# Mixer scores with one 128-row stationary operand, and the small steps of a threshold search on GpSimd

## Chip, cores and metric

One core of a Trainium2 chip runs the whole program in one launch. The metric is the device time of one execution in microseconds, as the median of several runs.

## What is computed

A decoder block on 1024 tokens of width 1024 (one layer, batch 1): a mixer of three kinds of attention, cross attention to 256 memory tokens, a gated MLP with a short convolution, and a last norm. The change lies in the mixer:

```
h = rmsnorm(x, norm_mix)
aq, ak, av, bq, bk, bv, cq, ck, cv, iq, ik, iw = split(h @ w_in)
A: 4 heads, two softmax maps of 64 columns each, minus lam times the second
B: 4 heads of 64 columns, dilated windows
C: indexer: score[t,s] = sum_h iw[t,h] * relu(iq[t,h] . ik[s] / 8)      (8 heads of 64 columns)
   the 256 best keys s <= t of each t are kept; 4 heads of 64 columns attend to them alone
x = x + concat(A, B, C) @ w_out
...
s = q . k * scale + bias[bucket(t - s)];   p = softmax(s);   o = p @ v
```

Products are made from float32 numbers split into a high part (float32r) and a low part, the rest: q = qh + ql, k = kh + kl.

## The kernel before, in words

`build_mixer` (L293) writes the mixer as strands, generators that yield pieces of work for an engine with an estimated duration. The class `Flow` (L60) runs them as a list schedule: of the work that is ready for an engine, the lowest rank goes first, and the order so found is the order in which the instructions are issued on TensorE, ScalarE, VectorE and GpSimd, and the transfers on SyncE. Each engine then runs its queue strictly in that order; a table `LAG` holds the estimated hand-over times. `Slots` are counters of free buffers, `Gate`s are events.

Projections: for each unit u (two heads, or one head of A with its two maps) `project_k`, `project_v` and `project_q` (L607, L629, L587) make the transposed keys, the values and the queries, in two halves of 512 tokens, each half from 24 matmuls with 512 moving columns (three passes, `mm3`, L174 to L176, for each of eight chunks). Keys of the next unit are projected beside the scores of this one (`kk_s` has two slots). ScalarE copies the high part out of PSUM, VectorE subtracts to get the low part. For the queries the transfers issued by SyncE (L158) build `qs`, whose 128 rows are, for each of the two heads, [high; low] of its 64 columns; `qh` keeps the high parts of both heads in their own rows. For the keys they build `kd`, [high; high] of each head; the low parts `kl` stay where VectorE wrote them, 64 rows a head.

Scores: `scores_mm` (L705) makes a chunk of up to 512 keys for 128 queries in two passes into one PSUM bank. The first, L709, takes `qs` against `kd` over 128 rows: qh.kh + ql.kh. The second, L710, takes 64 rows of `qh` against 64 rows of `kl`: qh.kl. It is used by the indexer (`index_chunk`, tile psi, 80 chunks) and by all heads (`scores_all`, tile pss, 192 chunks). `index_keys` (L666) has one head of keys, and makes its copies in both halves of the rows itself.

Evacuation: VectorE adds the bias strip and finds the maximum in one pass (`evacuate`, shown as CUSTOM_DVE, with its accumulator read as `nm`), ScalarE takes the exponentials; `turn_all` transposes, `values_all` multiplies with the values.

Search: `selection` (L775) finds the 256th best score of each row bit by bit, 16 bits of the high halves and 16 of the low ones, for two sets of row blocks: blocks 2 to 5 count on VectorE (suffix d, four counts a bit), blocks 6 and 7 on ScalarE (suffix a, two counts a bit). After the counts of a bit three small VectorE instructions on 128x4 or 128x2 elements set the next threshold (`sel_g`, `sel_thr`, then `sel_lo`). `rank()` paces the search to an end at 505 us of the schedule's own clock. Where masks are ready, the scores of units 6 and 7 add them by a third matmul (L895).

GpSimd has, in this part, the low parts of the weights (`wl`, 128x512, L117, the line of every recorded strand) in the same order of issue.

Of the kernel before, what the change touches and what calls it, by code (L numbers as in the profile page):

```python
# [14 lines left out]
F32 = mybir.dt.float32  # L15
F32R = mybir.dt.float32r
# [8 lines left out]
P = 128  # L25
# [34 lines left out]
class Flow:  # L60
    """Decides the order in which the engines get their instructions: a list schedule over a small model
    of the engines. A strand is a generator that yields (engine, us, emit[, rank]) for work, a time to
    let pass, a Gate to wait for, or Slots to take one of; the lowest rank goes first. Work that several engines
    can do goes to the one that would be done with it first."""
# [86 lines left out]
def trunk(ctx, tc, a, out):  # L151
# [3 lines left out]
    def rdma(dst, src):  # L155
        """Copies float32r bits."""
        f = lambda t: t.bitcast(F32) if t.dtype == F32R else t
        nc.sync.dma_start(f(dst), f(src))  # L158
# [5 lines left out]
    # ---------------------------------------------------------------- helpers  # L164
# [13 lines left out]
    def load_w(pool, w, c, n=P, parts=1, eng=nc.gpsimd):  # L178
        """128 columns of a weight matrix, split: lists of [128, n] by chunk of rows."""
# [13 lines left out]
    def rsqrt(v, n, between):  # L193
        """1 / sqrt(v) for a tile of n columns, with other work between its steps."""
# [30 lines left out]
    def transposed_split(src, dst_h, dst_l, col, trp, tag="tr"):  # L225
        """src [128 rows, 1024] into dst[:, chunk, col:col+128], split."""
        for q in range(2):
            ps = trp.tile([P, 4, P], F32, tag=tag, name="tr")
            for j in range(4):
                c = (4 * q + j) * P  # L230
                nc.tensor.transpose(ps[:, j, :], src[:, c : c + P], ident)
            dh = dst_h[:, 4 * q : 4 * q + 4, col : col + P]
            nc.scalar.activation(dh, ps, AF.Copy)
            nc.vector.tensor_tensor(dst_l[:, 4 * q : 4 * q + 4, col : col + P], ps, dh.bitcast(F32), OP.subtract)

    # -------------------------------------------------------------- constants
# [8 lines left out]
    # DRAM scratch  # L245
# [12 lines left out]
    def w_half(w, half, name, pool, stp):  # L258
        """512 columns of a weight matrix, split."""
# [33 lines left out]
    def build_mixer():  # L293
# [5 lines left out]
        vt_s, pt_s, o_s, t_s, w_s, st_s = Slots(2), Slots(2), Slots(2), Slots(2), Slots(3), Slots(2)  # L299
        go, put, open_ = flow.go, flow.put, flow.open  # L300

        def move(us, *fs, rank=None):
            """Transfers as strand work."""
# [13 lines left out]
        def rstd_ops(ss, width, n, res):  # L317
            """The steps of 1 / sqrt(ss / width + eps) as strand work."""
# [19 lines left out]
        # ------------------------------------------------ weights of columns  # L338
# [53 lines left out]
        # ------------------------------------------------ rows, normalised and transposed  # L392
# [12 lines left out]
        class Rows:  # L405
            """Blocks of rows that share the steps to their inverse norms."""
# [10 lines left out]
        def row_block(rows, j, t):  # L417
            """A block of rows: loaded, normalised, transposed, split."""
# [58 lines left out]
        def all_rows():  # L477
            """Memory first: its projection fills the time that the tokens need."""
# [8 lines left out]
        def keep_clock():  # L487
            """Fills the array's pauses before the first long run of products, so that its clock stays up."""
# [10 lines left out]
        # ------------------------------------------------ bias vectors by distance, lambda  # L499
# [46 lines left out]
        def load_strips():  # L546
            """The biases of a head, skewed by row: 128 copies a row apart by one."""
# [23 lines left out]
        # ------------------------------------------------ projections  # L571
# [15 lines left out]
        def project_q(key, u, scale):  # L587
            """Transposed projection of two heads, by half: high parts, and [high; low] of each head."""
            hd = heads[u]

            def finish(half, ps):
                yield vt_s
                qh = hp.tile([P, 512], F32R, tag="qh", name="qh", bufs=3)
# [8 lines left out]
                hd.q[half] = (qh, qs)  # L602
# [4 lines left out]
        def project_k(key, u):  # L607
            """Transposed projection of two heads: low parts, and [high; high] of each head."""
            hd = heads[u]

            def finish(half, ps):
                yield vt_s
                sl = slice(512 * half, 512 * half + 512)
                kh = pp.tile([P, 512], F32R, tag="vt", name="kh")
                yield ACT, act(512), partial(nc.scalar.activation, kh, ps, AF.Copy)
                yield DVE, dve(512), partial(nc.vector.tensor_tensor, hd.kl[:, sl], ps, kh.bitcast(F32), OP.subtract)
                put(pj_s)
                r = [slice(0, 64), slice(64, 128)]
                yield from move(1.46, *(copy(hd.kd[r[x], m, sl], kh[r[m]]) for m in range(2) for x in range(2)))
                put(vt_s)  # L620
                hd.k = hd.kl, (hd.kd[:, 0], hd.kd[:, 1])
# [3 lines left out]
            hd.kl = hp.tile([P, S], F32R, tag="kl", name="kl")  # L625
# [3 lines left out]
        def project_v(key, u):  # L629
            """Values in their natural layout, [high | low] for each head."""  # L630
# [34 lines left out]
        # ------------------------------------------------ indexer  # L665
        def index_keys():  # L666
            hd = heads["ik"]

            def finish(half, ps):
                yield vt_s  # L670
                kl, kh = hd.kl, hd.kd[:, 0]
# [7 lines left out]
                hd.k = kl, (kh, kh)  # L679
# [15 lines left out]
            hd.kl = hp.tile([P, S], F32R, tag="kl", name="ikl")  # L695
# [3 lines left out]
        def chunks_of(n):  # L699
            """Columns by bank, none under half of one where that can be helped."""  # L700
# [4 lines left out]
        def scores_mm(ps, q, k, m, qb, c0, n, stop=True):  # L705
            qh, qs = q[qb // 4]
            c = slice(qb % 4 * P, qb % 4 * P + P)
            r = slice(64 * m, 64 * m + 64)
            nc.tensor.matmul(ps[:, :n], qs[:, m, c], k[1][m][:, c0 : c0 + n], start=True, stop=False)  # L709
            nc.tensor.matmul(ps[:, :n], qh[r, c], k[0][r, c0 : c0 + n], start=False, stop=stop)  # L710
# [43 lines left out]
        # ------------------------------------------------ the 256 best keys of each row  # L754
# [5 lines left out]
        def keys(b):  # L760
            """Ordered 16-bit keys of the scores: high halves, low halves (as stored)."""
# [13 lines left out]
        def selection(blocks, on_act, end):  # L775
            """The 256th best score of each row, bit by bit: of the high halves, then of the low ones of
            the scores that share that high half. mask[b] = 1 where a key is not among the 256 best."""
# [14 lines left out]
            def search(src, c, bits):  # L792
                for bit in range(bits - 1, -1, -1):
# [9 lines left out]
                    for f in (partial(nc.vector.tensor_tensor, g, cnt, need, OP.is_le if on_act else OP.is_ge),  # L803
                              partial(nc.vector.tensor_scalar, g, g, 0.5, float(1 << bit), OP.subtract, OP.mult),
                              partial(nc.vector.tensor_tensor, c, c, g, OP.add)):
                        yield DVE, 0.073, f, rank()
# [8 lines left out]
            # keys above; low halves, turned where the sign is negative  # L815
# [34 lines left out]
        # ------------------------------------------------ attention  # L850
# [93 lines left out]
        def groups(n):  # L944
            """Blocks to turn, a group to a bank: (which of the two tiles, block of keys)."""
# [140 lines left out]
        # ------------------------------------------------ memory  # L1086
# [128 lines left out]
        def out_weights():  # L1215
            """The output projection's weights and the heads, as soon as there is room."""
# [53 lines left out]
    # ------------------------------------- output projection, cross attention  # L1270
    # The order of the work is found by a list schedule. Three products of matrices follow each other: of the
    # heads and w_out, of w_mq and the tokens, of the attention to the memory and w_mo, each in Winograd's form
    # of Strassen's: seven products of half the size in place of eight, in four chunks of the inner dimension.
    # Ranks are the number of the chunk that the work is for.
# [51 lines left out]
    def after(n):  # L1326
        """A gate that opens when something has happened n times."""
# [13 lines left out]
    # -------- products  # L1341
# [3 lines left out]
    # Shapes of the operands: left and right blocks, and the sum that takes a block's place before.  # L1345
# [29 lines left out]
    class Product:  # L1375
        """One of the three; `needs` gives the gates that an operand waits for, `kept` does with the result of a
        product for 128 rows what there is to do."""
# [75 lines left out]
    class Sums:  # L1453
        """What is kept of the products: two rows of X for 128 rows, to which they are added."""
# [40 lines left out]
    # -------- norms of rows  # L1495
# [20 lines left out]
    def normed_rows(ts, X, done, gain, xn_of, save, turned, rank, scale=1.0):  # L1516
        """Rows, each with its norm, as soon as they are done; saved as they are, turned when they are normed."""
# [22 lines left out]
    def turned_rows(xn, dst, t, hits, slots, rank):  # L1540
        """xn [128 rows, 1024] into dst[:, chunk, its columns]."""
# [23 lines left out]
    # -------- output projection  # L1565
# [35 lines left out]
    # -------- tokens, normalised, and their queries, scaled  # L1601
# [6 lines left out]
    def load_weights(w, to, gates, j, rank):  # L1608
        """Half of the rows of a matrix, in two transfers."""
# [119 lines left out]
    # -------- attention to the memory  # L1729
# [151 lines left out]
    # -------- its projection  # L1881
# [44 lines left out]
    # -------- norm of the tokens for the MLP  # L1926
# [57 lines left out]
    # ------------------------------------------------------------ gated MLP  # L1984
# [7 lines left out]
    # An operand is made in three stages: the sum (in the place of a block that is done with), its high and its low part.  # L1992
# [18 lines left out]
    # Work beside the products, in the order of its emission, some of it after each product.  # L2011
# [621 lines left out]
```

## Time and profile before

| | us |
|---|---|
| median of 3 runs | 1907.18 |
| lowest and highest run | 1897.14, 1908.43 |
| span of the profiled execution | 1898.1 |

The page gives for the profiled execution its span, from the first to the last instruction; it lies within 1 us of the fastest run, so nothing that could be told stands around it, and the median of the runs is 9.1 us more. Stretches below are in us from the span's start. Busy times of TensorE count from a matmul's start to its modelled end, so that a wait for weights inside this time counts as busy; start-to-start times of matmuls show it.

### The profile page before, as it was taken

Reading aid. Unit: us, or ns where it says so; the run is one execution under the profiler, and the core shown is the slowest. Engines: PE = TensorE matmul, PEld = TensorE weight load, DVE = VectorE, ACT = ScalarE, POOL = GpSimd, SP = SyncE. Lnnn points to the kernel's source line nnn. Section 1 sums busy time; section 2 is a strip of 40 time slices with the busy share of each in tenths; the row PEclk is TensorE's granted clock in tenths of the full one; section 3 lists DMA queues with packets and bytes.
Section 4 is the critical chain, followed back from the end, with each engine's and each line's share of the span. In section 5 each row is a group of like instructions: output and inputs, shape, how many; then the busy total and the mean of one; then the engine's idle time right before and its main releaser. Section 6 shows DMA issues by size and latency. Waiting matters only on the chain. (4 is left out here: it accounts for less than half of the span.)

```text
span 1898.1 us, 23427 instructions
## 1 busy us (share of the span) xinstructions
PE 1743.3 (92%) x7836; PEld 1344.3 (71%) x7836; DVE 1542.9 (81%) x2759; ACT 941.8 (50%) x1847; POOL 910.5 (48%) x595
## 2 busy tenths in 40 slices
PE   7899999999999999987999987999999999799987
PEld 7655766776677776766778765777777777577865
DVE  8445899999988756898986899777776777899997
ACT  5344567667675555535554535434334343353333
POOL 3201111101111012564643556877788877778896
PEclk8999999999999999989899988999999999999988
DMA  8563222322323228505023111122222221752202
GB/s 264 153 185 79 68 61 73 78 59 64 79 75 103 62 69 270 183 33 189 3 107 116 56 67 45 56 89 68 77 78 67 78 77 46 288 176 69 89 1 89
DMA packets 146682, 184.50 MB, mean 97 GB/s; under 512 B 10921, under 2 KB 99329, under 8 KB 146561
## 3 DMA queue, kind: packets, MB, share of 16 engines
q1 hardware_dynamic: 146561, 183.00, 30.8%
q8 instruction: 62, 1.02, 0.2%
q14 instruction: 59, 0.48, 0.1%
HBM read 126.81 MB, written 41.74 MB: 89 GB/s over the span
## 5 line engine op out<-in xcount | busy, mean ns | idle before, releaser
L117 POOL TENSOR_TENSOR wl<-st,wh 128x512 fp32r<-128x512 f32 (+1 forms) x58 | 77.1, 1330 | 540.0 <-ACT wh L117 467.6
L174 PE MATMUL up<-T,wo 128*128 128x512 f32 x616 | 248.6, 404 | 27.4 <-DVE ta L2100 26.3
L175 PE MATMUL up<-T,wo 128*128 128x512 f32 x616 | 246.2, 400 | 7.0 <-DVE T L1990 7.0
L176 PE MATMUL up<-T,wo 128*128 128x512 f32 x616 | 245.6, 399 | 0.0
L174 PE MATMUL pj<-h1T,wh 128*128 128x512 f32 (+1 forms) x464 | 204.4, 441 | 0.0
L2016 DVE SCALAR_TENSOR_TENSOR ring<-ring,convv 128x1023 f32<-128x1023 f32 x88 | 155.3, 1765 | 43.9 <-issue 33.8
L1996 POOL TENSOR_TENSOR wst<-wst 128x512 f32<-128x512 f32 x82 | 146.3, 1784 | 87.2 <-DVE wo L1990 85.6
L176 PE MATMUL pj<-h1T,wl 128*128 128x512 f32 (+1 forms) x464 | 184.5, 398 | 0.0
L175 PE MATMUL pj<-h1T,wh 128*128 128x512 f32 (+1 forms) x464 | 184.4, 397 | 0.0
L1998 ACT ACTIVATE wo<-wst 128x512 fp32r<-128x512 f32 x144 | 87.8, 625 | 171.8 <-POOL wst L1996 169.2
L174 PEld LDWEIGHTS up<-T,wo 128*128 128x128 f32 x616 | 118.0, 192 | 64.0 <-issue 32.3
L174 PE MATMUL pr<-operands 128*128 128x512 f32 x336 | 141.0, 420 | 21.9 <-DVE x L117 12.6
L175 PE MATMUL pr<-operands 128*128 128x512 f32 x336 | 138.9, 413 | 5.9 <-DVE operands L1302 5.3
L1990 POOL TENSOR_TENSOR wo<-wst,wo 128x512 fp32r<-128x512 f32 x81 | 141.8, 1750 | 4.6 <-ACT wo L1998 4.6
L175 PEld LDWEIGHTS up<-T,wo 128*128 128x128 f32 x616 | 118.3, 192 | 33.0 <-DVE T L1990 6.4
L176 PE MATMUL pr<-operands 128*128 128x512 f32 x336 | 137.6, 410 | 0.0
L176 PEld LDWEIGHTS up<-T,wo 128*128 128x128 f32 x616 | 118.5, 192 | 26.8
L174 PE MATMUL dn<-db,da 128*128 128x512 f32 x280 | 113.9, 407 | 15.1 <-ACT u L2521 4.5
L175 PE MATMUL dn<-db,da 128*128 128x512 f32 x280 | 113.3, 405 | 11.9 <-POOL db L1990 10.3
L117 ACT ACTIVATE s<-s,nm 128x128 f32<-128x128 f32 (+7 forms) x128 | 98.6, 771 | 44.5 <-DVE nm L117 41.7
L176 PE MATMUL dn<-db,da 128*128 128x512 f32 x280 | 112.6, 402 | 0.6 <-POOL da L1990 0.6
L174 PEld LDWEIGHTS pj<-h1T,wh 128*128 128x128 f32 (+1 forms) x464 | 88.0, 190 | 32.8 <-issue 16.6
(342 smaller groups left out, 4731.8 us busy)
## 6 DMA issues: line engine op xcount, KB each, us to landing
wst<-in_w_up_dram SPq DMA_DIRECT2D x44, 512.0 KB, 3.8
st<-in_w_in_dram SPq DMA_DIRECT2D x56, 256.0 KB, 2.9
act<-ring SPq DMA_DIRECT2D x22, 512.0 KB, 3.0
raw<-act SPq DMA_DIRECT2D x40, 256.0 KB, 5.7
score<-in_w_mkv_dram SPq DMA_DIRECT2D x32, 256.0 KB, 3.0
kd<-kh SPq DMA_DIRECT2D x64, 128.0 KB, 2.4
skew<-vr_d SPq DMA_DIRECT2D x12, 576.0 KB, 11.0
qs<-qh SPq DMA_DIRECT2D x48, 128.0 KB, 2.4
```

The costliest lines, as they stand in the source:

```text
L117: op[2]()
L174: nc.tensor.matmul(ps, lh, rh, start=start, stop=False)
L175: nc.tensor.matmul(ps, lh, rl, start=False, stop=False)
L176: nc.tensor.matmul(ps, ll, rh, start=False, stop=stop)
L1990: eng.tensor_tensor(s[:, 1], src, s[:, 0].bitcast(F32), OP.subtract)
L1996: e.tensor_tensor(src, a, b, op)
L1998: nc.scalar.activation(s[:, 0], src, AF.Copy)
L2016: f()
```

## The change

Both passes of the scores take `qs` as stationary operand. The low parts of the keys are kept like the high ones, [low; low] of each head, built by four more transfers for each half; ql.kl is now added, too. `qh` is no longer kept beyond the transfers that read it: it and `kh` share a tag of two buffers, `kt`, with slots of their own. The three small steps of the search on VectorE become four on GpSimd (difference, clamp to -1 and 0, scale and shift, add). The scratch for descriptors of GpSimd's own transfers is set to 4096 bytes, which makes room in SBUF for the wider `kl`. The diff, with what is only comments left out:

```diff
-        vt_s, pt_s, o_s, t_s, w_s, st_s = Slots(2), Slots(2), Slots(2), Slots(2), Slots(3), Slots(2)
+        vt_s, pt_s, o_s, t_s, w_s, st_s, kt_s = Slots(2), Slots(2), Slots(2), Slots(2), Slots(3), Slots(2), Slots(2)
...
         def project_q(key, u, scale):
...
                 yield vt_s
-                qh = hp.tile([P, 512], F32R, tag="qh", name="qh", bufs=3)
+                yield kt_s
+                qh = hp.tile([P, 512], F32R, tag="kt", name="qh")
...
                 put(vt_s)
-                hd.q[half] = (qh, qs)
+                put(kt_s)
+                hd.q[half] = qs
...
         def project_k(key, u):
...
                 yield vt_s
+                yield kt_s
                 sl = slice(512 * half, 512 * half + 512)
-                kh = pp.tile([P, 512], F32R, tag="vt", name="kh")
+                kh = hp.tile([P, 512], F32R, tag="kt", name="kh")
+                kl = pp.tile([P, 512], F32R, tag="vt", name="kl")
                 yield ACT, act(512), partial(nc.scalar.activation, kh, ps, AF.Copy)
-                yield DVE, dve(512), partial(nc.vector.tensor_tensor, hd.kl[:, sl], ps, kh.bitcast(F32), OP.subtract)
+                yield DVE, dve(512), partial(nc.vector.tensor_tensor, kl, ps, kh.bitcast(F32), OP.subtract)
                 put(pj_s)
                 r = [slice(0, 64), slice(64, 128)]
-                yield from move(1.46, *(copy(hd.kd[r[x], m, sl], kh[r[m]]) for m in range(2) for x in range(2)))
+                yield from move(2.92, *(copy(to[r[x], m, sl], of[r[m]]) for to, of in ((hd.kd, kh), (hd.kl, kl)) for m in range(2) for x in range(2)))
                 put(vt_s)
-                hd.k = hd.kl, (hd.kd[:, 0], hd.kd[:, 1])
+                put(kt_s)
+                hd.k = (hd.kl[:, 0], hd.kl[:, 1]), (hd.kd[:, 0], hd.kd[:, 1])
                 open_(hd.kr[half])
 
             yield kk_s
-            hd.kl = hp.tile([P, S], F32R, tag="kl", name="kl")
+            hd.kl = hp.tile([P, 2, S], F32R, tag="kl", name="kl")
...
         def scores_mm(ps, q, k, m, qb, c0, n, stop=True):
-            qh, qs = q[qb // 4]
-            c = slice(qb % 4 * P, qb % 4 * P + P)
-            r = slice(64 * m, 64 * m + 64)
-            nc.tensor.matmul(ps[:, :n], qs[:, m, c], k[1][m][:, c0 : c0 + n], start=True, stop=False)
-            nc.tensor.matmul(ps[:, :n], qh[r, c], k[0][r, c0 : c0 + n], start=False, stop=stop)
+            both = q[qb // 4][:, m, qb % 4 * P : qb % 4 * P + P]
+            nc.tensor.matmul(ps[:, :n], both, k[1][m][:, c0 : c0 + n], start=True, stop=False)
+            nc.tensor.matmul(ps[:, :n], both, k[0][m][:, c0 : c0 + n], start=False, stop=stop)
...
-                    for f in (partial(nc.vector.tensor_tensor, g, cnt, need, OP.is_le if on_act else OP.is_ge),
-                              partial(nc.vector.tensor_scalar, g, g, 0.5, float(1 << bit), OP.subtract, OP.mult),
-                              partial(nc.vector.tensor_tensor, c, c, g, OP.add)):
-                        yield DVE, 0.073, f, rank()
+                    for f in (partial(nc.gpsimd.tensor_tensor, g, need if on_act else cnt, cnt if on_act else need, OP.subtract),
+                              partial(nc.gpsimd.tensor_scalar, g, g, 0.0, -1.0, OP.min, OP.max),
+                              partial(nc.gpsimd.tensor_scalar, g, g, float(1 << bit), 0.5 * (1 << bit), OP.mult, OP.add),
+                              partial(nc.gpsimd.tensor_tensor, c, c, g, OP.add)):
+                        yield POOL, 0.11, f, rank()
...
-    nc = bacc.Bacc("TRN2", target_bir_lowering=False, num_devices=1)
+    nc = bacc.Bacc("TRN2", target_bir_lowering=False, num_devices=1, dynamic_dma_scratch_size=4096)
```

The index keys change only in the shape of `kl` and in how it is handed on. In the three places below names are tiles, and the number before a name is a source line.

TensorE, at the first score of the indexer, among the projection of the next queries, before:

```order
L176 MATMUL pj<-h1T_0_108,wl 128x512
L709 MATMUL psi<-ikh,qs 128x384
L710 MATMUL psi<-ikl,qh 128x384
L174 MATMUL pj<-h1T_0_108,wh 128x512
L175 MATMUL pj<-h1T_1_109,wh 128x512
```

and now:

```order
L176 MATMUL pj<-h1T_0_108,wl 128x512
L712 MATMUL psi<-ikh,qs 128x384
L713 MATMUL psi<-ikl,qs 128x384
L174 MATMUL pj<-h1T_0_108,wh 128x512
L175 MATMUL pj<-h1T_1_109,wh 128x512
```

The place and the number of matmuls are the same; the second reads `qs`, 128 rows, in place of `qh`, 64 rows.

VectorE, early in the search, beside the attention of the first unit, before (score_873 to score_876 are the four counted blocks, first to last):

```order
L117 TENSOR_SCALAR score_876,sel_cnt_d<-mask_145,sel_thr_d 128x768
L117 TENSOR_TENSOR sel_g_a<-sel_cnt_a,sel_need_a 128x2
L117 TENSOR_TENSOR sel_g_d<-sel_cnt_d,sel_need_d 128x4
L117 TENSOR_SCALAR sel_g_a<-sel_g_a 128x2
L117 TENSOR_SCALAR sel_g_d<-sel_g_d 128x4
L117 TENSOR_TENSOR sel_thr_a<-sel_thr_a,sel_g_a 128x2
L117 TENSOR_TENSOR sel_thr_d<-sel_thr_d,sel_g_d 128x4
L117 TENSOR_SCALAR score_873,sel_cnt_d<-mask_142,sel_thr_d 128x384
L117 TENSOR_SCALAR score_874,sel_cnt_d<-mask_143,sel_thr_d 128x512
```

and now, beside the same unit:

```order
L117 TENSOR_SCALAR score_876,sel_cnt_d<-mask_145,sel_thr_d 128x768
L117 TENSOR_SCALAR score_873,sel_cnt_d<-mask_142,sel_thr_d 128x384
L117 SCALAR_TENSOR_TENSOR oa<-av,rl,ta 128x128
L117 TENSOR_SCALAR score_874,sel_cnt_d<-mask_143,sel_thr_d 128x512
L117 TENSOR_TENSOR ptl<-trp,pth 128x512 x2
```

The six small steps are gone, and the last count of a bit stands right before the first of the next. On GpSimd there stands in their place, with the weight splits among them:

```order
L117 TENSOR_TENSOR wl<-st,wh 128x512
L117 TENSOR_TENSOR sel_g_d<-sel_cnt_d,sel_need_d 128x4
L117 TENSOR_SCALAR sel_g_d<-sel_g_d 128x4 x2
L117 TENSOR_TENSOR sel_thr_d<-sel_thr_d,sel_g_d 128x4
L117 TENSOR_TENSOR sel_g_a<-sel_need_a,sel_cnt_a 128x2
L117 TENSOR_SCALAR sel_g_a<-sel_g_a 128x2 x2
L117 TENSOR_TENSOR sel_thr_a<-sel_thr_a,sel_g_a 128x2
```

SyncE's transfers for the first keys, before:

```order
L158 DMA kd<-kh 64x512 x4
L117 DMA st<-in_w_in_dram 128x4x128
L158 DMA kd<-kh 64x512 x4
L117 DMA st<-in_w_in_dram 128x4x128
L158 DMA qs<-qh 64x512 x2
L158 DMA qs<-ql 64x512 x2
```

and now:

```order
L158 DMA kd<-kh 64x512 x4
L158 DMA kl<-kl 64x512 x4
L117 DMA st<-in_w_in_dram 128x4x128
L158 DMA kd<-kh 64x512 x4
L158 DMA kl<-kl 64x512 x4
L117 DMA st<-in_w_in_dram 128x4x128
L158 DMA qs<-qh 64x512 x2
L158 DMA qs<-ql 64x512 x2
```

Four transfers of the low parts stand between those of the high parts and the next weights.

## Rows read from the trace of the kernel before

**Rows 1.** Busy time by stretch: engine sums (instructions), TensorE clock, DMA share, GB/s
```profile
core 0 of [0], span 1898.1 us
...
88.00:206.00 118.00, 114.94 (x379) 68.13 (x378) 65.95 (x110) 49.54 (x98) 15.72 (x15) 0.97 0.46 127
206.00:515.00 309.00, 296.66 (x1377) 218.82 (x1375) 288.76 (x984) 208.33 (x506) 37.33 (x29) 0.98 0.27 69
515.00:605.00 90.00, 89.93 (x451) 68.13 (x450) 76.70 (x193) 61.34 (x124) 11.70 (x8) 1.00 0.36 94
605.00:765.00 160.00, 158.48 (x830) 119.00 (x829) 107.47 (x289) 86.31 (x188) 25.26 (x19) 0.99 0.41 125
765.00:1898.20 1133.20, 1007.79 (x4356) 805.24 (x4354) 945.27 (x1057) 494.83 (x855) 791.81 (x487) 0.95 0.26 89
```

**Rows 2.** Timeline from 121 to 124 us, TensorE's matmuls (PE) and weight loads (PEld)
```profile
121.39 0.50 PE L709 MATMUL psi<-ikh,qs 128*128 128x512 f32 x1
...
121.82 0.50 PE L710 MATMUL psi<-ikl,qh 64*128 64x512 f32 x1
...
122.25 0.50 PE L174 MATMUL pj<-h1T,wh 128*128 128x512 f32 x1
...
122.58 0.39 PE L175 MATMUL pj<-h1T,wh 128*128 128x512 f32 x1
122.59 0.19 PEld L176 LDWEIGHTS pj<-h1T,wl 128*128 128x128 f32 x1
122.82 0.39 PE L176 MATMUL pj<-h1T,wl 128*128 128x512 f32 x1
...
123.05 0.40 PE L709 MATMUL psi<-ikh,qs 128*128 128x512 f32 x1
123.37 0.18 PEld L710 LDWEIGHTS psi<-ikl,qh 64*128 64x128 f32 x1 [0.36 <-issue]
123.37 0.49 PE L710 MATMUL psi<-ikl,qh 64*128 64x512 f32 x1
...
123.80 0.50 PE L174 MATMUL pj<-h1T,wh 128*128 128x512 f32 x1
```

**Rows 3.** First passes of the scores, L709, by stretch: matmuls (count), weight loads (count)
```profile
88.00:206.00 118.00, 31.50 (x79) 15.16 (x79) 0.97 0.46 127
206.00:515.00 309.00, 40.30 (x103) 19.52 (x103) 0.98 0.27 69
515.00:605.00 90.00, 11.75 (x31) 5.65 (x30) 1.00 0.36 94
605.00:765.00 160.00, 23.95 (x60) 11.46 (x60) 0.99 0.41 125
```

**Rows 4.** VectorE's time in instructions on sel_g_a, then on sel_g_d, second stretch
```profile
206.00:515.00 309.00, 19.90 (x84) 0.98 0.27 69
...
206.00:515.00 309.00, 21.22 (x95) 0.98 0.27 69
```

**Rows 5.** Timeline: two places of the search, on GpSimd (POOL), VectorE, ScalarE
```profile
260.31 1.29 POOL L117 TENSOR_TENSOR wl<-st,wh 128x512 fp32r<-128x512 f32 x1 [7.62 <-ACT wh L117]
...
260.36 1.27 DVE L117 TENSOR_SCALAR sel_g_d<-sel_g_d 128x4 f32<-128x4 f32 x1
...
302.48 0.15 DVE L117 TENSOR_TENSOR sel_thr_a<-sel_thr_a,sel_g_a 128x2 f32<-128x2 f32 x1
...
302.72 1.04 ACT L117 ACTIVATE score<-mask,sel_thr_a 128x896 int16<-128x896 int16 x1 [1.17 <-DVE sel_g_d L117]
```

**Rows 6.** Groups of GpSimd instructions by line and shape: busy, mean ns, idle before
```profile
L117 POOL TENSOR_TENSOR wl<-st,wh 128x288 fp32r<-128x288 f32 x2 | 2.3, 1141 | 2.6 <-ACT wh L117 2.6
...
masks.py:199 POOL TENSOR_SCALAR_AFFINE_SELECT ident<-ident 128x128 f32<-128x128 f32 x1 | 0.3, 295 | 0.0
...
L830 POOL MEMSET sel_lo_d<- 128x4 f32 x1 | 0.1, 103 | 0.0
```

**Rows 7.** Part 6 of the page: transfers by tile, count, KB each, us to landing
```profile
kd<-kh SPq DMA_DIRECT2D x64, 128.0 KB, 2.4
```

More of the change, by code (lines that the diff above doesn't have):

```diff
@@ L670, in finish @@
                 yield vt_s
-                kl, kh = hd.kl, hd.kd[:, 0]
+                kl, kh = hd.kl[:, 0], hd.kd[:, 0]
                 sl = slice(512 * half, 512 * half + 512)
@@ L678, in finish @@
                 put(pj_s)
-                hd.k = kl, (kh, kh)
+                hd.k = (kl, kl), (kh, kh)
                 yield tr_s
@@ L694, in index_keys @@
             yield kk_s
-            hd.kl = hp.tile([P, S], F32R, tag="kl", name="ikl")
+            hd.kl = hp.tile([P, 2, S], F32R, tag="kl", name="ikl")
             hd.kd = hp.tile([P, 2, S], F32R, tag="kd", name="ikh")
```

## Prediction, made before the run

> **What bounds the kernel now.** I read the busy time by stretches first, then the order of the instructions on TensorE inside a stretch, then the rows of the two other engines that the change touches. The span is 1898.1 us [rows 1]. The mixer's part that the change touches runs from about 88 to 765 us; there TensorE is busy 115 of 118, 297 of 309, 90 of 90 and 158 of 160 us, and no other engine comes near it except VectorE in the second stretch, with 289 of 309 [rows 1]. That second stretch is the search for the 256 best keys beside the attention of the first heads. So three stretches are bound by TensorE alone, and one by TensorE and VectorE nearly alike. From 765 us on nothing is changed; that part I carry over at its 1133 us [rows 1].
>
> But TensorE is not always computing while it counts as busy. Plain matmuls with 512 moving columns start 0.23 to 0.24 us apart (122.58, 122.82, 123.05), and the next weights are loaded while the last matmul runs (the load at 122.59 beside the matmul of 122.58) [rows 2]. At a score it is otherwise. The second pass, L710, has a 64-row stationary operand; its load starts only at 123.37, 0.32 us after the first pass at 123.05, and the engine waits "issue", for nothing that the profile shows. The matmul behind it starts 0.43 us after it, at 123.80 [rows 2]. A pair so takes 0.75 us where two plain matmuls take 0.46. Where pairs follow each other both halves take 0.43: 121.39, 121.82, 122.25 [rows 2], 0.86 us.
>
> **The change part by part.**
>
> *Scores.* Both passes get the same 128-row operand, so neither the entry into 64 rows nor the exit from it is left. The number of matmuls and their columns stay. A pair that follows other work saves 0.75 - 0.46 = 0.29 us, one that follows a pair 0.86 - 0.46 = 0.40. Of the 272 pairs in the trace 83 stand right behind another one. That is 83 x 0.40 + 189 x 0.29 = 33 + 55 = 88 us, 0.32 a pair. Narrow chunks save about as much as wide ones, since what goes is the wait and not the columns. By the pairs of each stretch (79, 103, 31 and 60 [rows 3]) it is 25, 33, 10 and 19 us.
>
> *The search's small steps.* 192 VectorE instructions go (32 bits, two searches, three each) and 256 come on GpSimd. In the second stretch they take 19.9 + 21.2 = 41.1 us of VectorE [rows 4], more than 192 undisturbed steps of 0.15 us would, because some are held up: beside GpSimd's weight split at 260.31 a step on 4 columns took 1.27 us, where the one at 302.48 took 0.15 [rows 5]. GpSimd is busy 37 of 309 us there [rows 1] and has room. What is new is a wait: the first count of a bit on VectorE waits for four steps on GpSimd in a row, and behind that count stand score evacuations, for which TensorE waits in turn. The trace has no such step on GpSimd. From below, a MEMSET of the same 128x4 takes 0.10 us; an AFFINE_SELECT of 128x128, 32 times as many elements, takes 0.30; from above, the nearest two-input row is the 128x288 one with 1.14 [rows 6]. I take 0.2, between the two small ones and near both, so a chain of four with its two hand-overs (0.09 us each, as from VectorE's step that ends at 302.63 to ScalarE's count at 302.72 [rows 5]) is 1.0 us. In the order of the changed kernel 4 of the 32 bits have nothing on VectorE between their last count and the next bit's first, and 8 have under 1 us of work there (0.64 on average, each instruction valued as in the trace); the others cover the chain. The stall is 4 x 1.0 + 8 x 0.36 = 7 us. With steps of 0.1 us it is about 3, with steps of 1.14 (a chain of 4.7) about 97, by the same list. The other search counts on ScalarE, busy 208 of 309 us [rows 1], and gains: its steps no longer stand in VectorE's queue.
>
> *Keys copied twice.* 64 more transfers of 128 KB go into SyncE's queue, four behind each group of four from kh. A transfer takes 2.4 us to land, and keys are projected one unit ahead of their scores [rows 7]. The low parts now wait for VectorE's subtraction, and the next weight load stands behind them. The queries' low parts have waited so in 24 places all along while TensorE stayed busy; I cost it at nothing. If that cover goes, it is one more landing of 2.4 us for each of 16 halves, at most 38 us. One buffer fewer for qh, and the smaller descriptor scratch, touch no instruction that waits: every transfer here is issued by SyncE. Zero, with either sign possible by a few us through the shifted order.
>
> *Sum.* First stretch: 25, and VectorE with 66 of 118 us leaves room. Second: TensorE loses 33, VectorE 41 - 7 = 34, so both come down alike and their idle shares stay; I take 28, because the 256 steps share GpSimd's queue, in order, with the 29 instructions that stand there now [rows 1]. Third: 10. Fourth: 18 of 19, the tail of the last heads being short chains. 25 + 28 + 10 + 18 = 81 us. From the span that gives 1898.1 - 81 = 1817; the median of the runs, 1907.2, stands 9 us above the span, so the median to expect is **1826 us**.
>
> **Two rules against it.** The load of L176 at 122.59 overlaps the matmul at 122.58, and both target all 128 rows [rows 2]. The Trainium skill says otherwise (TensorE: Matmul & The Clock Gate, Part 3, The mechanism): weight loads overlap matmuls in flight only when their row groups differ. By that rule the second pass, with the same rows, would show its load in full; here the trace disagrees, and only a small chance is left for it.
>
> GpSimd's split and a VectorE step on SBUF exclude each other at 260.36 [rows 5]. The Trainium skill (GPSIMD Engine Reference, Key points) has the reason: the two share SBUF interfaces, with contention where VectorE uses a 2-port mode or two SBUF inputs. By that rule 256 new GpSimd steps may each hold VectorE up; the trace agrees on the mechanism. What it costs by rows: 256 x 0.2 us = 51 us if each step met such a VectorE instruction, more than the 41 us that VectorE is rid of; since only some do, it counts under the first rival.
>
> **The rivals.**
>
> *The search gets slower on GpSimd.* Steps of 0.4 us, or waits behind a weight split that itself waits for ScalarE, make the chain 2.5 us. By the same list that is 35 us of stall in place of 7, so VectorE comes down by 6 us and the second stretch by about as much; 25 + 6 + 10 + 18 = 59, 1848 us. For it: GpSimd's queue is in order and its splits take 1.3 us. Against it: it is idle seven eighths of the stretch [rows 1].
>
> *The gain is lost behind the mixer.* The memory's weights and the output projection's are loaded in its last stretch, at a DMA share of 0.41 [rows 1], and the transfers don't speed up. If the fourth stretch gives back what it saved, 25 + 28 + 10 = 63, 1844 us. Against it: TensorE is busy 158 of 160 us there, so nothing is late now.
>
> *The second pass does not get cheaper.* With both loads shown, a pair is 2 x (0.23 + 0.19) = 0.84 us, as now. VectorE's relief alone can give at most TensorE's idle 12 us of the second stretch: 1895 to 1907.
>
> *Slower than before.* Place: the first count of each bit on VectorE. If a GpSimd step costs 1.4 us with its own hand-over, the chain is 6 us, and the 32 bits have 54 us of cover in all: 32 x 6 - 54 = 138 us of stall. VectorE then needs 289 - 41 + 138 = 386 us in the second stretch, plus the 20 that it idles now, so that stretch grows by 97 us; the others save 53: 1951 us. It decides from a chain of some 5.2 us on. For it stands only the row of 1.14 us; against it the two small rows [rows 6].
>
> **How the numbers follow.** The forecast 0.62, the slow search 0.21, the loss behind the mixer 0.10, no cheaper pass 0.04, slower 0.03. The first three are all faster by over 1%, about what a measurement can tell from no change, so faster is 0.93, within 1% 0.04, slower 0.03. The likeliest case itself spans 1812 to 1842. For 8 in 10 the range runs from 1803 (all 88 us on TensorE, 41 on VectorE, and some of the idle time of the second stretch) to 1860, beyond the slow search by a chain of 3 us (48 us of stall, the second stretch saving nothing: 25 + 10 + 18 = 53, 1854).
>
> **What would show it.** Right: the load of the second pass overlapping the first, starts 0.23 us apart at 512 columns; the mixer's end near 684 us in place of 765; VectorE's sum without the 41 us; GpSimd steps of 0.2 us. Wrong: idle time before the search's counts on VectorE with GpSimd as releaser, over 20 us in all; weight loads on SyncE late behind the copies of the low parts; idle time on TensorE that ends with VectorE between 200 and 450 us; or a stage behind the mixer that is longer than 1133 us.

## The result, and the profile after

The changed kernel takes 1827.58 us (median of 4 runs, 1825.33 to 1829.2); the one before took 1906.77 beside it. The ratio is 0.960, 95% interval [0.955, 0.964]: 4% faster. Forecast were 1826 us and a range of 1803 to 1860. The profiled execution spans 1823.5 us, 74.6 less than before; the sum had said 81.

The first lines of the page, of before and then of after, TensorE and VectorE first to look at:

```profile
PE 1743.3 (92%) x7836; PEld 1344.3 (71%) x7836; DVE 1542.9 (81%) x2759; ACT 941.8 (50%) x1847; POOL 910.5 (48%) x595
```

```profile
span 1823.5 us, 23627 instructions
...
PE 1649.0 (90%) x7836; PEld 1335.9 (73%) x7836; DVE 1511.5 (83%) x2567; ACT 937.5 (51%) x1847; POOL 966.3 (53%) x851
```

TensorE (PE; its weight loads are PEld) issues as many matmuls and as many weight loads as before and is busy 94 us less. VectorE (DVE) is busy 31 us less, not 41. Their shares of the span hardly moved: neither engine became free.

Busy time by stretch of after, cut at the same first passes of the scores as [rows 1], within one (columns: stretch and length; PE, PEld, DVE, ACT, POOL with instructions; clock, DMA share, GB/s):

```profile
88.00:176.60 88.60, 84.74 (x387) 70.28 (x386) 65.83 (x111) 48.53 (x100) 15.59 (x15) 0.98 0.66 183
176.60:468.80 292.20, 269.12 (x1403) 219.92 (x1402) 273.22 (x824) 215.93 (x526) 91.25 (x281) 0.98 0.35 89
468.80:542.30 73.50, 70.88 (x403) 59.35 (x402) 64.94 (x162) 50.06 (x101) 11.44 (x12) 1.00 0.43 115
542.30:691.00 148.70, 144.23 (x841) 118.48 (x840) 102.94 (x284) 85.84 (x189) 24.82 (x20) 1.00 0.50 150
691.00:1823.60 1132.60, 1004.86 (x4357) 803.20 (x4356) 946.69 (x1058) 495.46 (x856) 794.28 (x487) 0.96 0.26 90
```

The stretches were 118, 309, 90, 160 and 1133.2 us [rows 1]; they lose 29.4, 16.8, 16.5, 11.3 and 0.6. Forecast were 25, 28, 10, 18 and 0. The last stretch is as long as it was, so nothing was given back there. Other work moved across the cuts (the third stretch has 403 matmuls, 451 before; the second 1403, 1377 before), so the third and the fourth are better taken together: 27.8 lost, 28 forecast. The search stretch is the one that falls short, and there both engines now stand idle: TensorE 23 us (12 before), VectorE 19 (20 before).

A score of the indexer on after's timeline, which answers to [rows 2]:

```profile
96.96 0.39 PE L712 MATMUL psi<-ikh,qs 128*128 128x512 f32 x1
96.96 0.19 PEld L713 LDWEIGHTS psi<-ikl,qs 128*128 128x128 f32 x1
97.19 0.39 PE L713 MATMUL psi<-ikl,qs 128*128 128x512 f32 x1
97.42 0.39 PE L174 MATMUL pj<-h1T,wh 128*128 128x512 f32 x1
```

The load of the second pass starts with the first pass (96.96) in place of 0.32 us behind it; a pair takes 97.42 - 96.96 = 0.46 us. The same weights are loaded a second time all the same, under the running matmul.

The small steps on GpSimd (counts; shortest, median and longest in ns; first and last start; forms):

```profile
L117 POOL TENSOR_SCALAR sel_g_d<-sel_g_d x64: 189/193/1097, 191.4 to 469.8; 128x4 f32<-128x4 f32 x64
L117 POOL TENSOR_TENSOR sel_g_d<-sel_cnt_d,sel_need_d x32: 192/201/1045, 191.1 to 469.2; 128x4 f32<-128x4 f32 x32
```

Waits of after, on the search and on the scores (engine, tile, line, what it waited for: us in all, times, longest):

```profile
POOL sel_g_d L117 <- DVE score L117: 74.0, 19, 11.9
...
POOL sel_g_a L117 <- ACT score L117: 34.2, 12, 6.2
...
ACT score L117 <- POOL sel_lo_a L117: 13.2, 6, 3.6
...
PE pss L712 <- DVE nm L117: 10.3, 10, 3.2
...
ACT score L117 <- POOL sel_thr_a L117: 8.8, 6, 4.6
...
DVE score L117 <- POOL sel_thr_d L117: 6.7, 10, 1.2
...
DVE score L117 <- POOL sel_lo_d L117: 3.7, 6, 1.2
```

VectorE waits 10.4 us for GpSimd (POOL) and ScalarE (ACT) 22.0, together 32.4. TensorE's matmuls wait 10.3 us for evacuated scores (`nm`); before it was 4.1:

```profile
PE pss L709 <- DVE nm L117: 4.1, 4, 1.4
```

One place of after shows how these waits arise:

```profile
257.68 0.19 ACT L117 ACTIVATION_READ_ACCUMULATOR score<-mask,sel_thr_a 128x1 f32 x1
...
258.22 1.27 POOL L117 TENSOR_TENSOR wl<-st,wh 128x512 fp32r<-128x512 f32 x1
...
261.25 0.08 DVE L117 DVE_READ_ACCUMULATOR score<-mask,sel_thr_d 128x1 f32 x1
...
261.47 0.20 POOL L117 TENSOR_TENSOR sel_g_d<-sel_cnt_d,sel_need_d 128x4 f32<-128x4 f32 x1 [1.98 <-DVE score L117]
...
262.31 0.20 POOL L117 TENSOR_TENSOR sel_thr_d<-sel_thr_d,sel_g_d 128x4 f32<-128x4 f32 x1
262.46 0.19 POOL L117 TENSOR_TENSOR sel_g_a<-sel_need_a,sel_cnt_a 128x2 f32<-128x2 f32 x1
...
262.54 0.61 DVE L117 TENSOR_SCALAR_CACHE_REDUCE score<-mask,sel_thr_d 128x384 int16<-128x384 int16 x1 [0.61 <-POOL sel_thr_d L117]
...
263.08 0.28 DVE L117 CUSTOM_DVE_ANT_0 s<-pss,strip 128x128 f32<-128x128 f32 x1
...
263.43 0.58 PE L712 MATMUL pss<-kd,qs 128*128 128x256 f32 x1 [3.24 <-DVE nm L117]
...
263.51 1.04 ACT L117 ACTIVATE score<-mask,sel_thr_a 128x896 int16<-128x896 int16 x1 [4.64 <-POOL sel_thr_a L117]
```

ScalarE's counts are ready at 257.87, but their step starts at 262.46. In GpSimd's queue a weight split and the step of the other search stand ahead of it, and that one waits for VectorE's counts. So one search waits for the other, and ScalarE stands 4.64 us. TensorE waits 3.24 us for the evacuation at 263.08, which stands behind VectorE's count at 262.54; of these 3.24 us that count's own wait for GpSimd makes 0.61. The steps themselves take 0.2 us but start some 0.28 us apart: from 261.47 to 262.51 the chain of four takes 1.04 us, and from the end of one count (261.33) to the start of the next (262.54) 1.2 us.

At the end of this wait TensorE is granted half its clock (0.50, which is 1.2 GHz), for 6.8 us:

```profile
264.90 0.63 PE L174 MATMUL pj<-h1T,wh 128*128 128x512 f32 x1
265.33 0.63 PE L175 MATMUL pj<-h1T,wh 128*128 128x512 f32 x1
```

```profile
263.00:269.80 6.80, 6.29 (x16) 4.93 (x17) 6.21 (x27) 6.18 (x16) 3.25 (x12) 0.50 0.44 105
```

In the 3.4 us before, it was busy 0.59 us. The clock falls twice more in the search stretch, at 327.9 and 392.7, each time behind a wait of TensorE (2.05 us to 326.88, 2.37 us to 391.61). At this level matmuls with 512 columns start 0.43 us apart (264.90, 265.33), and 0.23 us apart at 2.4 GHz (96.96, 97.19, 97.42). A wait of TensorE can so cost more than its own length.

The copies of the low parts land as fast as those of the high parts (issues of after: tile, count, KB each, us to landing):

```profile
kd<-kh SPq DMA_DIRECT2D x64, 128.0 KB, 2.3
kl<-kl SPq DMA_DIRECT2D x64, 128.0 KB, 2.4
```

### The profile page after: what moved, and what is told of

It reads as the page before. It is cut to its first block, busy times and chain, and to the rows that moved or that the text cites. A ratio compares the mean times of both kernels' runs of the same rounds, so it can differ in the third digit from the quotient of the medians.

```text
span 1823.5 us, 23627 instructions
## 1 busy us (share of the span) xinstructions
PE 1649.0 (90%) x7836; PEld 1335.9 (73%) x7836; DVE 1511.5 (83%) x2567; ACT 937.5 (51%) x1847; POOL 966.3 (53%) x851
## 5 line engine op out<-in xcount | busy, mean ns | idle before, releaser
L174 PE MATMUL up<-T,wo 128*128 128x512 f32 x616 | 247.8, 402 | 28.9 <-DVE ta L2104 27.8
L174 PE MATMUL pj<-h1T,wh 128*128 128x512 f32 (+1 forms) x464 | 192.7, 415 | 0.0
L175 PE MATMUL pj<-h1T,wh 128*128 128x512 f32 (+1 forms) x464 | 183.7, 396 | 0.0
L175 PE MATMUL dn<-db,da 128*128 128x512 f32 x280 | 113.5, 405 | 12.4 <-POOL db L1994 10.8
L1994 POOL TENSOR_TENSOR da<-raw,da 128x512 fp32r<-128x512 f32 x60 | 97.6, 1640 | 24.5 <-ACT da L2002 24.5
```

The costliest lines, as they stand in the source:

```text
L174: nc.tensor.matmul(ps, lh, rh, start=start, stop=False)
L175: nc.tensor.matmul(ps, lh, rl, start=False, stop=False)
L1994: eng.tensor_tensor(s[:, 1], src, s[:, 0].bitcast(F32), OP.subtract)
```

## Experiments

Each time stands beside runs of the kernel before on the same chip; the ratio is to those. The second number of interest is the length of the search stretch, from the indexer's last score (the 80th first pass) to the 183rd first pass, in each kernel's own trace: 309.9 us before and 292.2 after.

**The scores alone, the search alone.** The first takes the changed kernel and puts the three VectorE steps back; the second takes the kernel before and only moves the steps.

```diff
-                    for f in (partial(nc.gpsimd.tensor_tensor, g, need if on_act else cnt, cnt if on_act else need, OP.subtract),
...
-                        yield POOL, 0.11, f, rank()
+                    for f in (partial(nc.vector.tensor_tensor, g, cnt, need, OP.is_le if on_act else OP.is_ge),
...
+                        yield DVE, 0.073, f, rank()
```

> The changed kernel with the search's small steps back on VectorE (three in place of four on GpSimd). Theory of the two bounds: TensorE alone sets the stretches without the search, so they keep their gain (30 us up to the last score of the indexer, about 10 from the first masked score on); in between VectorE, with 289 of 309 us, bounds the search, and of the 34 us gained there about 15 stay: 1907 - 55 = 1852 us. Rival, TensorE alone bounds everything and GpSimd's part is worth nothing: 1828 us as in the changed kernel, within 5.

> The kernel before with the four steps of the search on GpSimd and nothing else changed. Theory of the two bounds: TensorE, 297 of 309 us busy in that stretch, keeps the bound; VectorE's sum falls by some 35 us and the time by 0 to 10: 1897 to 1907 us. Rival, VectorE was the bound of the search and the relief is what made the changed kernel faster there: 20 us or more, under 1887. Rival, the waits on GpSimd cost more than they give: over 1910.

Scores alone: 1822.24 us (1818.66 to 1825.66), ratio 0.955 [0.946, 0.963], not the 1852 of the theory. Search alone: 1905.21, ratio 0.999 [0.994, 1.003]. So the whole gain is the scores', and the search's move gives nothing by itself, nor on top of them. Search alone leaves VectorE 1511.6 us busy, the 31 less that the changed kernel has too, and its search stretch is 314.1 us long. The same stretch with the scores alone:

```profile
177.50:458.70 281.20, 263.72 (x1376) 213.73 (x1374) 278.12 (x989) 206.97 (x505) 38.40 (x29) 0.98 0.36 89
```

It takes 281.2 us, 28.7 less than before, and VectorE is busy in 278.1 of them: there, not before, VectorE is the bound. In the changed kernel it is busy in 273.2 of 292.2, and the stretch is 11 us longer. About half of that is work done earlier: TensorE has 27 matmuls more in it (1403, here 1376), 5.4 us of busy time, and the scores alone lose 6 us in the next two stretches (224.8 us to the last score, 219.2 in the changed kernel). What is left, some 5 us, is about what the medians differ by: the move frees VectorE, and the waits take more than that back. ScalarE's waits for the search with the scores alone, and TensorE's for `nm`:

```profile
ACT score L117 <- DVE sel_thr_a L117: 5.0, 3, 3.4
ACT score L117 <- DVE sel_lo_a L117: 4.3, 4, 1.7
ACT score L117 <- DVE sel_g_d L117: 2.8, 1, 2.8
ACT s L117 <- DVE sel_g_d L117: 1.3, 2, 1.1
...
PE pss L712 <- DVE nm L117: 9.2, 12, 2.5
```

ScalarE's are 13.4 us, 22.0 in the changed kernel. TensorE's matmuls wait 9.2 us for `nm` here too: most of that wait comes with the cheaper scores, not with GpSimd.

**What makes the second pass cheap.** The kernel before, with 128 rows in its second pass; the operand is not shared and the keys are not copied.

```diff
-            nc.tensor.matmul(ps[:, :n], qh[r, c], k[0][r, c0 : c0 + n], start=False, stop=stop)
+            nc.tensor.matmul(ps[:, :n], qh[:, c], k[0][:, c0 : c0 + n], start=False, stop=stop)
```

> The kernel before with one edit: the second pass takes all 128 rows of qh and of kl, so its stationary operand is another one than the first pass's, with the same number of rows, and no copy of the low parts is added. The scores so get the other head's product of high and low parts too; time is all it is for. Theory, the 64 rows are the cost: as with the scores' change alone, 1852 us, pairs with 0.23 us between starts at 512 columns. Rival, the operand that the passes share is what saves: pairs as before, 1907 us. If the copies of the low parts cost anything, this kernel is faster than the scores' change alone by it.

1828.18 us, ratio 0.958 [0.950, 0.965]. Its timeline:

```profile
122.85 0.39 PE L708 MATMUL psi<-ikh,qs 128*128 128x512 f32 x1
122.85 0.19 PEld L709 LDWEIGHTS psi<-ikl,qh 128*128 128x128 f32 x1
123.07 0.39 PE L709 MATMUL psi<-ikl,qh 128*128 128x512 f32 x1
...
123.30 0.40 PE L708 MATMUL psi<-ikh,qs 128*128 128x512 f32 x1
```

0.45 us a pair with two different operands. What cost 0.75 and 0.86 us was the second pass's 64 rows among matmuls of 128; that both passes have one operand is not needed. Whether it is the change of rows or the 64 rows as such is not shown: no kernel here has two 64-row matmuls in a row. As this kernel has none of the 64 copies and is no faster than the scores alone, the copies cost nothing that shows. It is in fact 6 us slower, with VectorE busy 1541.4 us (1534.8 with the scores alone); why is open.

**A longer chain on GpSimd.** The first two steps of each bit are issued three times, in the same order: four steps more in each of the 64 chains.

```diff
+                    def thrice(f):
+                        for _ in range(3):
+                            f()
...
+                    for f in (partial(thrice, partial(nc.gpsimd.tensor_tensor, g, need if on_act else cnt, cnt if on_act else need, OP.subtract)),
+                              partial(thrice, partial(nc.gpsimd.tensor_scalar, g, g, 0.0, -1.0, OP.min, OP.max)),
```

> The changed kernel with the first two of the four steps on GpSimd issued three times each (same result, eight instructions in a chain in place of four, the order of all other instructions as it was). With 0.2 us an instruction the chain goes from 1.0 to 1.8 us. Theory of the prediction: VectorE's wait for GpSimd goes from 10 us to some 23, and the time up by 8 to 13 us: 1836 to 1841. Rival, the chain is covered by what stands between: within 3 us of 1828. Rival, the wait grows by the full 0.8 us in each of 64 chains: 1879.

1868.74 us, ratio 0.980 [0.972, 0.987]: 41 us more than the changed kernel, above the 1836 to 1841 of the theory. A chain, the search stretch and the waits:

```profile
259.18 0.77 POOL L808 TENSOR_TENSOR sel_g_d<-sel_cnt_d,sel_need_d 128x4 f32<-128x4 f32 x3 [1.03 <-DVE ri L117]
...
261.13 0.20 POOL L117 TENSOR_TENSOR sel_thr_d<-sel_thr_d,sel_g_d 128x4 f32<-128x4 f32 x1
```

```profile
176.10:510.50 334.40, 282.80 (x1403) 230.88 (x1402) 277.57 (x824) 216.73 (x525) 139.32 (x533) 0.93 0.31 78
```

```profile
ACT score L117 <- POOL sel_thr_a L117: 29.2, 13, 6.9
ACT score L117 <- POOL sel_lo_a L117: 29.1, 9, 7.6
DVE score L117 <- POOL sel_thr_d L117: 21.2, 14, 2.3
DVE score L117 <- POOL sel_lo_d L117: 15.0, 12, 2.4
```

The chain takes 2.15 us (259.18 to 261.33) in place of 1.04: the steps start 0.28 us apart, so 1.1 us were added and not the 0.8 expected, some 71 us to all the chains together. The waits are 94.5 us in place of 32.4, 62 of the 71 us more: hardly anything covers the chains. The time grows by 41 us. Not all of that is the waits themselves: the mean clock of the stretch is 0.93 (0.98 in the changed kernel), which makes 47 us at half the clock in place of 12, and by the starts 0.43 and 0.23 us apart that costs, as an estimate, up to 16 us.

**Which of the two searches.** The changed kernel again, then only ScalarE's steps on GpSimd, then only VectorE's own. The edit puts the three VectorE steps above under `else` of `if on_act`, or of `if not on_act`.

> The changed kernel once more, as the measure for the three others on this chip: 1823 to 1832 us.

> The changed kernel with only the steps of the search that counts on ScalarE left on GpSimd; those of the search that counts on VectorE are three instructions on VectorE again. Theory now: what ate the relief is GpSimd's queue in order. Steps for ScalarE's counts stand behind steps that wait for VectorE's counts, so ScalarE waits for VectorE through GpSimd (22 us), and VectorE itself waits 10 us. Here both waits go: ScalarE's wait for its thresholds under 10 us, VectorE's for GpSimd none, VectorE's sum some 12 us higher than in the changed kernel; 1812 to 1822 us. Rival, VectorE's sum is the bound: halfway between the changed kernel (1828) and the scores alone (1822), about 1825.

> The other half: the steps of the search that counts on VectorE on GpSimd, those for ScalarE's counts on VectorE. Theory: VectorE's wait for GpSimd stays near 10 us, ScalarE waits some 10 us for VectorE as with the scores' change alone; 1820 to 1828 us, above the other half. Rival, the sum is the bound: no difference between the two halves.

1826.73 (1826.06 to 1828.62), 1822.13 (1818.51 to 1824.98) and 1827.6 (1824.06 to 1829.54); ratios 0.961 [0.956, 0.965], 0.958 [0.954, 0.962], 0.961 [0.956, 0.965]. The intervals overlap; none is better than the scores alone. By the runs themselves, of one session, ScalarE's steps alone are 4.6 us faster than both searches on GpSimd. ScalarE then waits 10.8 us for GpSimd, not 22.0, and VectorE's counts not at all. With VectorE's steps alone, VectorE waits 8.1 us for GpSimd, and ScalarE 22.8 us for its own steps on VectorE, where some 10 were expected: a long wait of ScalarE does not need GpSimd's queue.

**What the schedule believes.** The table counts 0.11 us for a GpSimd step that takes 0.19 to 0.20 (0.26 in a chain, 1.04 / 4), so it puts the next count too close behind the chain. The edit is one number; it changes the order on all engines.

```diff
-                        yield POOL, 0.11, f, rank()
+                        yield POOL, 0.2, f, rank()
```

> The changed kernel with one number changed: the schedule counts 0.2 us for a step on GpSimd, as measured, in place of 0.11, so it puts 0.36 us more of other work between a bit's last count and the next bit's first. Theory, the waits come from a schedule that believes the chain shorter than it is: the waits of VectorE and ScalarE for GpSimd (10 and 22 us) fall by half, 1815 to 1823 us. Rival, the waits come from queues in order that no table sees: the same waits, 1825 to 1831 us.

> The changed kernel with 0.10 us in place of 0.11 us counted for a GpSimd step in the schedule: a difference that means nothing against the measured 0.19 to 0.20 us, but gives another order. If f3 was faster because the schedule knows the chain's true length, this one is like the changed kernel, 1824 to 1829 us, and its waits for GpSimd are as long (ScalarE some 22 us, VectorE some 10 us). If f3 was a lucky order, this and the next one scatter by as much as f3 did, anywhere from 1814 to 1835 us.

> The same with 0.12 us. Known length: 1823 to 1829 us with waits for GpSimd of about 30 us in all. Luck of the order: anywhere from 1814 to 1835 us, and not with the waits.

> The same with 0.30 us, more than a step takes. If what counts is that the schedule leaves the chain enough time, the waits for GpSimd fall below f3's (14.6 us on ScalarE, 7.3 us on VectorE) and the time is 1808 to 1817 us. If 0.2 us was right because it is true, a longer one only moves counts later: 1814 to 1822 us. If it was luck: 1814 to 1835 us.

| counted | time, us (runs) | ratio to before | waits for GpSimd, ScalarE + VectorE, us | search stretch, us |
|---|---|---|---|---|
| 0.10 | 1837.40 (1834.51 to 1840.21) | 0.966 [0.961, 0.971] | 26.6 + 16.1 = 42.7 | 301.3 |
| 0.11 | 1826.73 (1826.06 to 1828.62) | 0.961 [0.956, 0.965] | 22.0 + 10.4 = 32.4 | 292.2 |
| 0.12 | 1824.53 (1821.26 to 1825.53) | 0.959 [0.954, 0.964] | 18.8 + 12.2 = 31.0 | 292.0 |
| 0.20 | 1814.42 (1811.09 to 1816.11) | 0.954 [0.950, 0.958] | 14.6 + 7.3 = 21.9 | 280.7 |
| 0.30 | 1810.88 (1809.39 to 1812.17) | 0.952 [0.946, 0.958] | 4.6 + 4.0 = 8.6 | 273.1 |

(The waits of the 0.11 row are those of the changed kernel's trace.) The two largest of the waits at 0.30, and its search stretch:

```profile
ACT score L117 <- POOL sel_thr_a L117: 4.3, 5, 2.2
...
DVE score L117 <- POOL sel_thr_d L117: 2.1, 4, 0.9
```

```profile
177.90:451.00 273.10, 258.55 (x1385) 212.78 (x1383) 262.63 (x798) 214.87 (x522) 94.38 (x273) 1.00 0.37 93
```

Time, waits and the stretch fall together. An order of its own makes a difference too: 0.10 and 0.12, which ought to mean nothing, lie 13 us apart, about as far as 0.11 from 0.20; the expectation that 0.10 would be like 0.11 fell. But these two differ by 12 us of the same waits, and 0.20 and 0.30 lie below all three others. TensorE's mean clock in the stretch is 0.98, 0.98, 0.97, 0.99 and 1.00 in the order of the table; reckoned as for the longer chain, it makes up to 5 us of the difference between 0.11 and 0.30. That the time goes with these waits where both searches are on GpSimd is seen here, and forced by the longer chain; that a table nearer the truth must give fewer is likely from five points, not settled. Of 0.20 and 0.30 it is 0.30 that is the nearer: `LAG` has no hand-over between GpSimd's own steps, so the schedule believes the chain of 1.04 us to be 0.80 or 1.20 us long. A spread of orders with equal waits wasn't tried.

**Only ScalarE's steps, counted at 0.2 us.**

> Only ScalarE's search has its steps on GpSimd, as in f1, and the schedule counts 0.2 us for each. By the known length ScalarE's waits for GpSimd (10.8 us in f1) fall and the time is 1813 to 1820 us; VectorE's search has no such wait. If the order alone makes such differences: 1814 to 1830 us.

1821.31 us (1819.31 to 1823.44), ratio 0.958 [0.953, 0.963]. ScalarE's waits for GpSimd fall from 10.8 to 5.8 us and the time doesn't follow, against the expectation of 1813 to 1820: VectorE, which has its own steps back, is busy in 279.4 of the search stretch's 283.8 us and so again the bound. VectorE's steps are worth 7 us on GpSimd against 1814.42 (counted at 0.20, too, in another session) and 10 against 1810.88 (the same session, counted at 0.30), once their chain is waited for less.

The best of these kernels is the one with 0.30 us. Against the scores alone it is 11 us faster by the runs themselves (1809.39 to 1812.17 against 1818.66 to 1825.66, of two sessions, between which the changed kernel moved by 0.9 us); the ratios, with the scatter of before in them, don't part the two.

## Why the prediction was right, and which step failed

*The pairs* (88 us, by stretch 25, 33, 10 and 19): right. 0.75 and 0.86 us became 0.46, TensorE is busy 94 us less, and the scores alone bring 1908.47 - 1822.24 = 86 us beside the same runs. That the pause belongs to the 64-row pass was argued from [rows 2]; the run with 128 rows shows it. The sum left out a part that [rows 2] has: the matmul behind a pair is itself followed after 0.33 us (122.25 to 122.58), not 0.23. The Trainium skill (TensorEngine Tiling (Array Packing), Key Properties) says that changing the tiling mode drains TensorE; if 64 rows among 128 are such a change, the traces agree, at 0.29 us for a pair among plain matmuls. Its rule that weight loads overlap matmuls only across row groups (the Trainium skill, TensorE: Matmul & The Clock Gate, Part 3, The mechanism) stays contradicted by the load at 96.96.

*VectorE's 41 us* [rows 4]: mis-sized. Its busy time fell by 31 with the search alone, and by 1534.8 - 1511.5 = 23 on top of the new scores. The rows added up durations that overlap; of before:

```profile
302.22 0.15 DVE L117 TENSOR_SCALAR sel_g_a<-sel_g_a 128x2 f32<-128x2 f32 x1
302.27 0.15 DVE L117 TENSOR_TENSOR sel_g_d<-sel_cnt_d,sel_need_d 128x4 f32<-128x4 f32 x1
```

The second starts 0.05 us behind the first, which lasts 0.15.

*"Both come down alike", 28 us in the search stretch*: the step that failed. It lost 17. The cheaper scores alone brought 28.7, with VectorE at 99%; with the move the stretch is 11 us longer, about half of it work moved forward. Idle shares did not stay: TensorE's idle time rose from 12 to 23 us, and idle time that ends with VectorE was one of the signs named for being wrong. That the forecast came within 2 us is in part luck. The other stretches gave 57.2 where 53 were forecast. And two errors nearly cancel: the sum was 6.4 us too large (81 for 74.6), and the median, taken to stand 9.1 us above the span, stands 4.1 us above it in after (1827.58, 1823.5).

*The chain on GpSimd*: 0.2 us a step right (0.19 to 0.20), but the steps start 0.28 us apart, so the chain is 1.2 us with its hand-overs and not 1.0; VectorE's stall of 7 us was 10.4. What was missed is the other search. *"ScalarE gains"* was wrong: it waits 22.0 us, as it did in the kernel before (22.5), where the scores alone leave 13.4. I had valued each search's chain alone, but both share one queue in order, as at 262.46. That is the first rival's mechanism ("waits behind a weight split") with a second cause, at half its price or less: 11 us off the stretch, some 5 off the time, where that rival took 22 of the 28. How much of ScalarE's 22.0 us is the shared queue is not shown: with ScalarE's steps alone on GpSimd 10.8 are left, but with its steps on VectorE and the other search's on GpSimd it is 22.8.

*GpSimd against VectorE's SBUF access*: no loss shows. The count of 128x768 takes 1008 ns on average after and 1005 before, though 256 steps were added. In [rows 5] the GpSimd instruction beside the held step lasted 1.29 us; the counts show no such hold from steps of 0.2 us.

*Keys' copies*, nothing: right; *the loss behind the mixer*: it didn't come, 1132.6 against 1133.2 us. *The slower rival* needed a chain of 5.2 us; it is 1.2.

## What to carry to other kernels

Count what an engine is rid of by the union of its busy time, and ask whether it is the bound after the other part of the change, not before. Work moved to an idle engine enters a queue in order: two independent chains on it can wait for each other's inputs, and a schedule that believes the chain too short can pay on the engines that wait. Time a chain from its first start to its last end, not by the sum of its steps. A matmul with 64 rows among full ones was not cheaper here but dearer (0.75 us a pair, 0.46 with full rows); look at the starts, not at the busy time.

## What was not expected

A one-number change of the schedule's table, 0.10 to 0.12 us for a step that takes 0.20, moved the time by 13 us (1837.40 to 1824.53): small costs in a planner's table are part of the kernel. And the same stationary operand in two matmuls in a row saves nothing by itself: weight loads number 7836 before and after, and two different operands run as fast (0.45 us a pair).
